# A two-layer diffusion trunk: layer 1's first modulation group is computed inside layer 0's MLP

## The chip, the cores and the metric

One core of one Trainium2 chip. The core has five engines that run at once, each through its own queue in order: TensorE (PE, matrix products into PSUM; its weight loads are shown as PEld), VectorE (DVE), ScalarE (ACT), GpSimd (POOL), and SyncE (SP), which here issues the DMAs. The metric is the device time of one execution in microseconds, median over runs.

## The reference, cut to what matters

Two layers. In each, six modulation vectors are computed from a small condition (one vector for the 1024 latent tokens, one for the 128 context tokens); they scale and shift two normalised inputs and gate two outputs. The mixer (four head groups: two kinds of attention, a gated delta net, a long convolution) comes first, then a squared-ReLU MLP.

```python
def trunk_layer(x, cond, P, mixer):
    mod = jnp.einsum('bd,de->be', jax.nn.silu(cond), P['w_ada']) + P['b_ada']
    sh1, sc1, gt1, sh2, sc2, gt2 = jnp.split(mod[:, None, :], 6, axis=-1)
    h = rms_norm(x, P['g_pre_mix']) * (1.0 + sc1) + sh1
    o, extra = mixer(h)
    x = x + gt1 * rms_norm(o, P['g_post_mix'])
    h = rms_norm(x, P['g_pre_mlp']) * (1.0 + sc2) + sh2
    m = jnp.einsum('blf,fd->bld', jnp.square(jax.nn.relu(jnp.einsum('bld,df->blf', h, P['mlp_w1']))), P['mlp_w2'])
    x = x + gt2 * rms_norm(m, P['g_post_mlp'])
    return x, extra
```

The model width is 1024, the MLP's 4096. `w_ada` is 1024 x 6144 for each layer. The modulation depends on the condition and the weights alone, so it can be computed at any time before it is used.

## The kernel before

**Modulation.** `ada(l, g)` computes a third of layer `l`'s modulation, group `g`: (sh1, sc1), (gt1, sh2) or (sc2, gt2). The 2048 columns of `w_ada` of a group are cut into four slices of 512. A group has eight steps, one for each 128 rows of `w_ada`. A step loads four tiles `wada` of 128 x 512 (256 KB each, line 392, on SP's queue) and makes four products with the condition `cst` (128 x 32) in float32. Product `h` writes partitions 32h to 32h+31 of one PSUM tile `ada`, and accumulates there over the eight steps. After the last step ScalarE copies the tile to `adarow` (L398), TensorE transposes it in four pieces to `adat` (L229), and VectorE adds the bias into `mod` (L406).

**Who runs the groups.** Layer 0's group 0 runs in the lead. The others run in the mixer: `adas()` inside `layer` waits until the input projections are done and then runs, step by step, the layer's groups 1 and 2, and in layer 0 also layer 1's group 0. `run_timed` weaves this with `rest()` (projections, hyena, attention) and `other()` (the gated delta net) by a virtual clock for each. In attention `S` is the first pass that finds each query's largest score (its maximum goes through DRAM, `mscr`, and back into `Q`), `ST` the scores for the weights, `den` the sums of the weights, `O` the weighted values. After attention comes the output projection, `op`.

**The MLP.** `mlp` works in blocks; a block has two slices of 128 of the 4096 hidden columns (`j`). It runs 15 blocks, and `mlp_last` does the sixteenth. A block loads `w1` and `w2` of its two slices (`load_cols` and `load_rows`, lines 251 and 241: each a stage tile of 256 KB in tag T, then a cast of its high part by ScalarE, L253 and L242, and of the rest by VectorE, L232). Its first half makes `hid` (24 products of 384 columns for each of six pieces), with ReLU and square by ScalarE and VectorE (L1821 to L1823); its second half makes `mo` (18 tiles of 512 columns, six products each), which VectorE adds to `acc` (L1839).

**Buffers.** SBUF tags used here: T, 4 buffers, the stage tiles of `w1` and `w2`, and the `wada` tiles; L, 8 buffers, which hold the `w1` of just one block; C, 5 buffers, where the `w2` of one block stand in layer 0. PSUM: P, 4 banks, for `mo`, `ada`, `adat` and most others; q and O, 2 each, for `hid`.

**What sets the order.** The program is traced as a list of instructions. A planner then orders each engine's instructions by that list's order and by a simulated timeline, takes a tile's buffer when an earlier tile of the tag is free, and adds the semaphores; each engine then runs its queue in that order. `with tc.issue_after(i)` makes what is traced in the block stand behind instruction `i` on the same engine; it adds no wait. `self.last` is the last product traced by `mm`.

Of the kernel before, what the change touches and what calls it, by code (L numbers as in the profile page):

```python
# [19 lines left out]
DEPTH = 2  # L20
# [138 lines left out]
def bc(ap, n):  # L159

    return ap.unsqueeze(len(ap.shape)).broadcast_to(list(ap.shape) + [n])


class Trunk:
# [220 lines left out]
    def ada(self, l, g, tag="T"):  # L385

        nc = self.nc
        ps = self.P(name="ada")
        for kt in range(8):
            for h in range(4):  # L390
                w = self.H(name="wada", tag=tag[h % len(tag)])
                i = nc.sync.dma_start(out=w, in_=self.I["w_ada"][l, kt, :, g * 2048 + h * 512:g * 2048 + (h + 1) * 512])
                self.mm(ps[32 * h:32 * h + 32, :], self.cst[:, kt], w, kt == 0, kt == 7)
            if l == g == 0:
                self.lead = i
            yield
        row = self.H(name="adarow")
        nc.scalar.copy(out=row, in_=ps)  # L398
        pt = self.P((4, 2, 2, 32), name="adat")
        for b in range(4):  # L400
            self.tr(pt[:, b], row[:, b * 128:(b + 1) * 128])

        for half in range(2):
            o = self.mod[l][:, g, half * 4:half * 4 + 4]
            b = self.bada[l].rearrange("p (g s h b) -> p g s h b", g=3, s=2, h=2)[:, g, :, half].rearrange("p s b -> p b s")
            nc.vector.tensor_tensor(out=o, in0=pt[:, :, :, half, 0:2], in1=bc(b, 2), op=ALU.add)  # L406
        yield
# [1397 lines left out]
    def mlp(self, l, hi, lo):  # L1805
        nc = self.nc
        acc = []
        for b in range(15):
            us, w1s, w2s = [], [], []
            for j in (2 * b, 2 * b + 1):  # L1810
                w1s.append(self.load_cols(self.I["w1"][l, j], "w1"))
                w2s.append(self.load_rows(self.I["w2"][l, j * 128:(j + 1) * 128], "w2", [self.small] * 2))
                us.append((self.W(dt=F32R, name="uh", tag=self.big), self.W(dt=F32R, name="ul", tag="C" if j % 2 else self.big)))
            for c0, n in NCH:
                s = slice(c0, c0 + n)
                for w1, (uh, ul) in zip(w1s, us):
                    ps = self.P(name="hid", tag="Q")
                    for k in range(8):
                        self.mm3(ps[:, :n], w1(k), [hi[k][:, s], lo[k][:, s]], k == 0, k == 7)
                    r = self.H(name="relu")  # L1820
                    nc.scalar.activation(out=r[:, :n], in_=ps[:, :n], func=AF.Relu)  # L1821
                    nc.vector.scalar_tensor_tensor(out=r[:, :n], in0=ps[:, :n], scalar=0.0, in1=r[:, :n], op0=ALU.max, op1=ALU.mult)  # L1822
                    nc.scalar.copy(out=uh[:, s], in_=r[:, :n])  # L1823
                    self.lo_of(ul[:, s], r[:, :n], uh[:, s])
                if b == 0 and c0 < 768:
                    yield
            if b == 0:
                acc = [self.W((1024,), name="acc", tag=self.big) for _ in range(9)]
            for t in range(9):
                ts = slice(t * 128, t * 128 + 128)  # L1830
                for n in range(2):
                    ns = slice(512 * n, 512 * n + 512)
                    ps = self.P(name="mo")
                    for j in range(2):
                        self.mm3(ps, [x[:, ts] for x in us[j]], [x[:, ns] for x in w2s[j]], j == 0, j == 1)
                    if b == 0:
                        nc.vector.tensor_copy(out=acc[t][:, ns], in_=ps)
                    else:
                        nc.vector.tensor_tensor(out=acc[t][:, ns], in0=acc[t][:, ns], in1=ps, op=ALU.add)  # L1839
            yield acc  # L1840
# [203 lines left out]
    def layer(self, l):  # L2044


        I, nc = self.I, self.nc
# [26 lines left out]
        w = self.first_weights(l)  # L2074
# [23 lines left out]
        g, be = self.gdn_shared(l, gab, self.gdn_tag)  # L2098
# [5 lines left out]
        def until(x):  # L2104
            while x not in self.done:
                yield 1

        def adas():
            yield from until("proj")
            for a in ((l, 1), (l, 2)) + (((l + 1, 0),) if l + 1 < DEPTH else ()):  # L2110
                for _ in self.ada(*a):
                    yield 5

# [21 lines left out]
        def ahead(g):  # L2135
            while True:
                with self.tc.high_priority(300):
                    t = next(g, "end")
                if t == "end":
                    return  # L2140
                yield t
        run_timed((rest(), 1.5), (ahead(other()), GD), (adas(), 1))
        self.small, self.other = R[0][-1], R[1][-1]
        op = self.out_proj(l, R[1])
# [19 lines left out]
        for ts in range(7):  # L2164
            g = op([ts])
            out = next(g)
# [3 lines left out]
        g = op([7, 8])  # L2170
        out = next(g)
        self.run((g, 1), (group(0, xs[0:3]), 1), (group(1, xs[3:6]), 1))
        g = self.mlp(l, hi, lo)
# [75 lines left out]
```

## Time and profile before

| | us |
|---|---|
| median of 3 runs | 3819.6 |
| lowest, highest | 3818.95, 3856.05 |
| the profiled execution | 3818.92 |
| its span, first to last instruction | 3817.1 |

Times in the rows are microseconds from the start of the span. Names such as `L213` are lines of the kernel before; L213 is the helper that makes all products, so products are told apart by their tiles. `x8` counts instructions; a float32 product counts as two matmul instructions, one of the fp32r kind (`hid`, `mo`, `pj`) as one. In brackets stands how long the engine had been idle, and for what. Layer 0's MLP runs about 1150 to 1850 us, layer 0's attention about 690 to 1005, layer 1's about 2600 to 2885.

### The profile page before, as it was taken

To read this page: it belongs to the slowest core of one execution; us is meant where nothing else is said; L and a number is where in the kernel's file an instruction comes from. 1 tells how busy PE (TensorE), PEld (TensorE's weight loads), DVE (VectorE), ACT (ScalarE), POOL (GpSimd) and SP (SyncE) were. 2 spreads that over 40 slices of the span, in tenths; PEclk is the share of its full clock that TensorE was granted. 3 is DMA by queue.
4 is the path that set the end of the run, shared out by engine and by line. 5 is a ranking of instruction groups with operands and counts; after the bars stand their busy time and mean duration, and the time that the engine had idled before them with its cause. 6 is when DMAs were issued, how large, how long until landed. Compare 5 with 4: busy or idle time off the path is not lost. (4 is left out here: it accounts for less than half of the span.)

```text
span 3817.1 us, 58820 instructions
## 1 busy us (share of the span) xinstructions
PE 3530.3 (92%) x22478; PEld 2940.8 (77%) x22478; DVE 2236.0 (59%) x4583; ACT 1367.0 (36%) x2972; POOL 710.1 (19%) x710
## 2 busy tenths in 40 slices
PE   7989888799899999999989798787989999999998
PEld 4879774366689999999968787545656899999997
DVE  5765567677645444444586674767774544444446
ACT  5434343265543122212364334323664422222112
POOL 1152531013420000000131633211143200000003
PEclk9998889799999999999999898897989999999999
DMA  5346476832421111111334465755414211111113
GB/s 203 115 115 158 137 266 201 240 84 60 141 86 48 42 45 44 35 44 45 100 104 129 112 151 151 262 185 167 101 40 138 72 45 45 45 45 45 39 39 122
DMA packets 364677, 405.40 MB, mean 106 GB/s; under 512 B 115816, under 2 KB 237158, under 8 KB 364395
## 3 DMA queue, kind: packets, MB, share of 16 engines
q1 hardware_dynamic: 364394, 401.63, 35.1%
q8 instruction: 177, 2.90, 0.3%
q14 instruction: 106, 0.86, 0.1%
HBM read 298.34 MB, written 103.19 MB: 105 GB/s over the span
## 5 line engine op out<-in xcount | busy, mean ns | idle before, releaser
L213 PE MATMUL hid<-hT,w1h 128*128 128x384 f32 x3072 | 786.6, 335 | 0.1
L213 PE MATMUL pj<-hT,wah 128*128 128x384 f32 x2112 | 575.8, 351 | 10.4 <-ACT wah L253 4.2
L1839 DVE TENSOR_TENSOR acc<-acc,mo 128x512 f32<-128x512 f32 x504 | 345.9, 686 | 391.9 <-PE mo L213 391.9
L213 PEld LDWEIGHTS hid<-hT,w1h 128*128 128x128 f32 x3072 | 557.6, 188 | 14.4 <-ACT h L481 1.1
L213 PE MATMUL hid<-hT,w1l 128*128 128x384 f32 x1536 | 514.1, 335 | 0.0
L213 PE MATMUL mo<-w2h,ul 128*128 128x512 f32 x1116 | 435.0, 392 | 0.0
L213 PE MATMUL mo<-w2h,uh 128*128 128x512 f32 x1080 | 422.7, 391 | 0.0
L213 PE MATMUL mo<-w2l,uh 128*128 128x512 f32 x1080 | 422.7, 391 | 0.0
L213 PEld LDWEIGHTS pj<-hT,wah 128*128 128x128 f32 x2112 | 396.3, 196 | 23.3 <-issue 7.5
L213 PE MATMUL pj<-hT,wal 128*128 128x384 f32 x1056 | 368.2, 349 | 0.7 <-DVE wal L232 0.7
L242 ACT CAST w2h<-w 128x512 fp32r<-128x512 f32 x128 | 70.3, 619 | 732.7 <-PE mo L213 728.5
L269 POOL TENSOR_TENSOR postr<-postr,mhalf 128x1 f32<-128x1 f32 x36 | 22.3, 622 | 1564.1 <-DVE postr L268 1563.7
L213 PEld LDWEIGHTS hid<-hT,w1l 128*128 128x128 f32 x1536 | 288.3, 188 | 2.5
L213 PEld LDWEIGHTS mo<-w2h,ul 128*128 128x128 f32 x1116 | 209.6, 188 | 46.1
L662 POOL TENSOR_TENSOR e<-e,e 128x512 f32<-128x512 f32 (+1 forms) x120 | 162.2, 1353 | 445.3 <-ACT e L651 267.4
L213 PEld LDWEIGHTS mo<-w2h,uh 128*128 128x128 f32 x1080 | 202.8, 188 | 37.5
L213 PEld LDWEIGHTS mo<-w2l,uh 128*128 128x128 f32 x1080 | 202.7, 188 | 36.5
L232 DVE TENSOR_TENSOR el<-e,eh 128x512 fp32r<-128x512 f32 (+1 forms) x252 | 202.3, 820 | 32.2 <-ACT eh L653 30.3
L213 PEld LDWEIGHTS pj<-hT,wal 128*128 128x128 f32 x1056 | 206.4, 195 | 4.6 <-issue 2.0
L1822 DVE SCALAR_TENSOR_TENSOR relu<-hid,relu 128x384 f32<-128x384 f32 x180 | 99.4, 553 | 167.2 <-ACT relu L1821 167.2
L213 PE MATMUL ada<-wada,cst 128*32 128x512 f32 x384 | 137.0, 688 | 46.9 <-DMA wada<-in_w_ada 46.7
L1821 ACT ACTIVATE relu<-hid 128x384 f32<-128x384 f32 x180 | 87.8, 488 | 184.8 <-PE hid L213 184.8
(502 smaller groups left out, 6318.1 us busy)
## 6 DMA issues: line engine op xcount, KB each, us to landing
w<-in_w SPq DMA_DIRECT2D x256, 256.0 KB
wada<-in_w_ada SPq DMA_DIRECT2D x192, 256.0 KB
wa<-in_wa SPq DMA_DIRECT2D x88, 256.0 KB
x<-xres SPq DMA_DIRECT2D x21, 512.0 KB
x<-in_x SPq DMA_DIRECT2D x18, 512.0 KB
Q<-rscr SPq DMA_DIRECT2D x32, 288.0 KB
o<-oscr SPq DMA_DIRECT2D x18, 512.0 KB
xres<-x SPq DMA_DIRECT2D x36, 256.0 KB
```

What stands on the lines that cost most here:

```text
L213: self.last = self.nc.tensor.matmul(out, l, r, start=start, stop=stop, skip_group_check=True)
L232: self.nc.vector.tensor_tensor(out=lo, in0=x, in1=hi.bitcast(F32), op=ALU.subtract)
L242: self.nc.scalar.copy(out=hi[:, q], in_=st)
L269: self.nc.gpsimd.tensor_tensor(out=out, in0=out, in1=self.bcs(self.mhalf[:out.shape[0]], out.shape), op=ALU.pow)
L662: self.nc.gpsimd.tensor_tensor(out=acc, in0=acc, in1=e, op=ALU.add)
L1821: nc.scalar.activation(out=r[:, :n], in_=ps[:, :n], func=AF.Relu)
L1822: nc.vector.scalar_tensor_tensor(out=r[:, :n], in0=ps[:, :n], scalar=0.0, in1=r[:, :n], op0=ALU.max, op1=ALU.mult)
L1839: nc.vector.tensor_tensor(out=acc[t][:, ns], in0=acc[t][:, ns], in1=ps, op=ALU.add)
```

## The change

Layer 1's group 0 leaves layer 0's mixer and goes into layer 0's MLP. There `beside` runs one step in each of the blocks 1 to 8: its four loads are traced at the opening of the block, behind the block's own loads; its four products in the middle, behind the block's last `hid`, the one of the fourth tile first and the other three behind it. At the opening of block 9 come the copy, the transposes and the adds. In layer 1 `beside` is empty. For all other groups `ada` now takes a step's four tiles and traces its four loads first and its four products after them, where before each load was followed by its product.

```diff
@@ ada(self, l, g, tag="T")
         for kt in range(8):
+            w = [self.H(name="wada", tag=tag[h % len(tag)]) for h in range(4)]
             for h in range(4):
-                w = self.H(name="wada", tag=tag[h % len(tag)])
-                i = nc.sync.dma_start(out=w, in_=self.I["w_ada"][l, kt, :, g * 2048 + h * 512:g * 2048 + (h + 1) * 512])
-                self.mm(ps[32 * h:32 * h + 32, :], self.cst[:, kt], w, kt == 0, kt == 7)
+                i = nc.sync.dma_start(out=w[h], in_=self.I["w_ada"][l, kt, :, g * 2048 + h * 512:g * 2048 + (h + 1) * 512])
+            if g == 0 and l:
+
+                yield
+                with self.tc.issue_after(self.last.ins):
+                    self.mm(ps[96:128, :], self.cst[:, kt], w[3], kt == 0, kt == 7)
+            with self.tc.issue_after(self.last.ins) if g == 0 and l else contextlib.nullcontext():
+                for h in range(3 if g == 0 and l else 4):
+                    self.mm(ps[32 * h:32 * h + 32, :], self.cst[:, kt], w[h], kt == 0, kt == 7)
             if l == g == 0:
                 self.lead = i
             yield
@@ mlp(self, l, hi, lo)
         acc = []
+        beside = self.ada(l + 1, 0) if l + 1 < DEPTH else iter(())
         for b in range(15):
...
+            if b:
+                next(beside, None)
             for c0, n in NCH:
...
+            if b:
+                next(beside, None)
             if b == 0:
                 acc = [self.W((1024,), name="acc", tag=self.big) for _ in range(9)]
@@ layer(self, l)
         def adas():
             yield from until("proj")
-            for a in ((l, 1), (l, 2)) + (((l + 1, 0),) if l + 1 < DEPTH else ()):
+            for a in ((l, 1), (l, 2)):
                 for _ in self.ada(*a):
                     yield 5
```

## Rows read from the trace of the kernel before

**Rows 1.** Page, busy time of each engine over the span.

```profile
PE 3530.3 (92%) x22478; PEld 2940.8 (77%) x22478; DVE 2236.0 (59%) x4583; ACT 1367.0 (36%) x2972; POOL 710.1 (19%) x710
```

**Rows 2.** Windows, layer 0's MLP: stretch, length, busy us, PEclk, DMA share, GB/s.

```profile
1300.00:1350.00 50.00, 50.00 (x254) 45.50 (x253) 23.82 (x38) 10.29 (x20) 0.00 (x0) 1.00 0.13 43
```

**Rows 3.** Waits, 1200 to 1300 us: total us, times, longest.

```profile
DVE acc L1839 <- PE mo L213: 28.7, 31, 1.8
```

**Rows 4.** Windows of `ada` alone: stretch, length, PE, PEld, ACT busy, PEclk, DMA, GB/s.

```profile
700.00:730.30 30.30, 9.34 (x25) 1.22 (x26) 0.00 (x0) 0.68 0.95 280
730.30:770.00 39.70, 18.58 (x40) 2.35 (x38) 0.58 (x1) 1.00 0.71 204
```

**Rows 5.** Waits of TensorE, 700 to 730.3 us.

```profile
PE ada L213 <- DMA wada<-in_w_ada: 6.1, 4, 4.2
```

**Rows 6.** Timeline of TensorE in layer 0's attention: start us, us, engine, line, operation.

```profile
756.40 1.05 PE L213 MATMUL ada<-wada,cst 128*32 128x512 f32 x2
757.38 0.62 PE L213 MATMUL S<-K,Q 96*128 96x384 f32 x2
```

**Rows 7.** Timeline of TensorE at the end of layer 1's projections.

```profile
2428.66 0.33 PE L213 MATMUL pj<-hT,wal 128*128 128x384 f32 x1
2428.83 0.51 PE L213 MATMUL pj<-hT,wah 128*128 128x384 f32 x2
2429.18 0.34 PE L213 MATMUL pj<-hT,wal 128*128 128x384 f32 x1
2429.44 1.06 PE L213 MATMUL ada<-wada,cst 128*32 128x512 f32 x8
```

**Rows 8.** Timeline of TensorE in layer 0's hyena.

```profile
650.22 1.06 PE L213 MATMUL ada<-wada,cst 128*32 128x512 f32 x8
651.21 1.13 PE L213 MATMUL iz<-Y,inv 128*128 128x256 f32 x4
```

**Rows 9.** Timeline of TensorE, the end of the group that moves.

```profile
767.98 0.66 PE L229 MATMUL adat<-ident,adarow 128*128 128x128 f32 x4 [0.31 <-ACT adarow L398]
```

**Rows 10.** By tile: ns min/median/max, first and last start us; each layer's attention.

```profile
L213 PE MATMUL S<-K,Q x100: 275/340/689, 687.0 to 851.0; 96*128 96x384 f32 x96, 96*128 96x128 f32 x4
...
L213 PE MATMUL den<-e,ones x528: 269/273/423, 730.3 to 1006.6; 128*32 128x128 f32 x176
...
L213 PE MATMUL op<-woh,oh x144: 387/389/473, 1005.1 to 1109.4; 128*128 128x512 f32 x144
...
L213 PE MATMUL S<-K,Q x100: 275/387/689, 2598.9 to 2732.4; 96*128 96x384 f32 x96, 96*128 96x128 f32 x4
...
L213 PE MATMUL den<-e,ones x528: 272/296/423, 2631.4 to 2886.2; 128*32 128x128 f32 x176
...
L213 PE MATMUL op<-woh,oh x144: 387/389/499, 2885.3 to 2994.5; 128*128 128x512 f32 x144
```

**Rows 11.** Timeline of ScalarE in one block of layer 0's MLP.

```profile
1320.94 2.19 ACT L242 CAST w2h<-w 128x512 fp32r<-128x512 f32 x4 [25.34 <-PE mo L213]
...
1341.13 0.62 ACT L253 CAST w1h<-w 128x512 fp32r<-128x512 f32 x1
```

**Rows 12.** Timeline of TensorE around the same block.

```profile
1305.24 0.51 PE L213 MATMUL hid<-hT,w1h 128*128 128x384 f32 x2
...
1321.65 0.51 PE L213 MATMUL hid<-hT,w1h 128*128 128x384 f32 x2
...
1343.00 0.39 PE L213 MATMUL mo<-w2h,uh 128*128 128x512 f32 x1
```

**Rows 13.** Timeline of SP's queue, the same block's issues.

```profile
1322.32 1.52 SPq L251 DMA_DIRECT2D w<-in_w  x2
...
1338.15 2.41 SPq L251 DMA_DIRECT2D w<-in_w  x2
```

**Rows 14.** Timeline of VectorE, adds of `acc` in the same block.

```profile
1345.96 0.69 DVE L1839 TENSOR_TENSOR acc<-acc,mo 128x512 f32<-128x512 f32 x1
1347.32 0.69 DVE L1839 TENSOR_TENSOR acc<-acc,mo 128x512 f32<-128x512 f32 x1 [0.67 <-PE mo L213]
```

## Prediction, made before the changed kernel was run

> **What bounds the kernel now.** I read the page first: TensorE is busy for 92% of the span [rows 1], so in most stages TensorE's own work is the time, and what is added there is paid. The question is where that holds, so I read the windows next. In the MLP of layer 0 a window of 50 us has TensorE busy for all 50 us, at the full clock (1.00 is 2.4 GHz), VectorE under half, ScalarE a fifth, DMA 0.13 [rows 2]. The list of waits of that stretch has no wait of TensorE at all; the others wait for it, VectorE's adds of `acc` for `mo` 31 times in 100 us, 1.8 us at most [rows 3]. One block is 144 products `hid` and 108 products `mo`, 252 together; at 254 in 50 us a block takes 49.6 us. So the MLP is a stream of TensorE work without a hole: any product that is put into it lengthens the kernel by its own length.
>
> The group that moves, layer 1's group 0, runs in layer 0's mixer between 700 and 770 us. The windows of its products alone give 9.34 + 18.58 = 27.9 us of TensorE [rows 4] for 32 products, 8 steps of 4 (a product here is two matmul instructions), and before 730 us TensorE stood 6.1 us waiting for their loads [rows 5]. Why 28 us for so little: the timeline shows products alone among attention's products, one (x2) taking from 756.40 to 757.38, 0.98 us [rows 6]. The four products of a step write four different quarters of the output's partitions, and where all four are queued together they share the array: x8 stands with 1.06 us, and the next product starts 0.99 us after the first [rows 7, 8]. So the same step costs about 1 us together and about 4 us one by one. That is the lever of this change.
>
> **What the change removes.** The 64 instructions, their 32 loads and the waits. Bounds: at most the whole of it, 27.9 + 6.1 + 0.66 for the four transposes [rows 4, 5, 9] = 34.7 us. To see how much of that sets the end, there is a twin: layer 1 runs the same attention with two groups only, both over before its first `S`. From the first `S` to the first `op` layer 0 takes 1005.1 - 687.0 = 318.1 us, layer 1 2885.3 - 2598.9 = 286.4 us [rows 10]: 31.7 us less. It splits at the first `den` and the last `S`. First `S` to first `den`: 43.3 against 32.5 us, 10.8 less. First `den` to last `S`: 120.7 against 101.0 us, 19.7 less. Last `S` to first `op`: 154.1 against 152.9. Of the group, 9.3 us of TensorE and 6.1 us of waiting lie in the first part, 18.6 us and the transposes in the second [rows 4, 5], so the twin's differences sit where the group sits. The second part is TensorE's own time and I count it as sure; in the first part TensorE also waits, DMA is at 0.95 [rows 4], and layer 1 may do it faster for another reason. So 19.7 us is the lower bound, 34.7 the upper, and I take 31, next to the twin. The diff also lets the remaining groups ask for four tiles at once before their four products; loads and products are on different queues and their order on each stays, so I put that at nothing; it is bounded by the 0.98 us of a lone product either way for each step, and nothing in the rows says which way.
>
> **What the change adds on TensorE.** Eight steps, one in each of blocks 1 to 8, behind the block's last `hid`. By then (below) all four tiles are there, so they go in one run. From a dense stream into it: the product before starts at 2429.18, the step at 2429.44; the same kind of product takes 0.17 us to the next (2428.66 to 2428.83), so 0.09 us is lost [rows 7]. Out of it 0.99 us [rows 8]. A step is 1.08 us, 8 steps 8.6 us. Block 9 adds four transposes of 0.66 us in all with a wait of about 0.3 us before them [rows 9]: 1 us. Together 9.6 us. The copy `adarow` and the two small adds `mod` lie on ScalarE and VectorE, which wait for TensorE in that stage (ScalarE once 25.3 us a block [rows 11]); without that cover they'd cost under 1 us. Lower bound of the cost 8 x 0.99 + 0.4 = 8.3 us; upper bound, products that don't share, 8 x (4 x 0.98 + 0.09) + 1 = 33 us. I take 9.6, since the rows with x8 are this very form.
>
> The row says that eight instructions take 1.06 us where two take 1.05 [rows 6 to 8], so four products cost no more than one. The Trainium skill ("TensorE: Matmul & The Clock Gate", Measured speedup vs the span model) gives less for four tiles, 3.07 times instead of 4. By that a step would be 4 x 0.98 / 3.07 = 1.28 us (my estimate from that page) and the sum 1.6 us more. The trace disagrees here and decides. The page "TensorEngine Tiling (Array Packing)" of the Trainium skill, Key Properties, says that a change of the tiling mode drains the engine, which speaks against 16 such changes inside a dense stream; this trace shows 0.09 us for the way in.
>
> **What the change adds on the queues.** A step takes all four buffers of tag T, which the MLP's own loads use. Before, in a block that begins with `hid` at 1321.65 [rows 12], ScalarE casts the last four `w2` tiles at 1320.94 [rows 11], the buffers come free, and SP loads the next block's `w1` at 1322.32 and a second pair of `w1` at 1338.15 [rows 13]. Now the step's four loads stand at 1322 instead. A pair of tiles issued at 1338.15 was there when its cast ran at 1341.13, 3.0 us later [rows 11, 13], so four are there by about 1330, 13 us ahead of the middle of the block at 1343.00 [rows 12]. The 32 loads move past nothing else on SP there; DMA is at 0.13 [rows 2], where around the group it is at 0.95 and 0.71 [rows 4]. What is late next: all eight loads for the next block wait for the products, so they start near 1344. The first pair of `w1` lands at about 1347, is cast, the second by about 1351, done near 1353. The next block's `hid` begins at 1321.65 + 49.6 = 1371, 18 us later. But before, a few `hid` of the next block stand already among `mo`: the first at 1305.24, that is 11.8 us after that block's middle (1343.00 - 49.6 = 1293.4) [rows 12]. For such early ones only 2 us are left. I count nothing, since the planner places them by when their weights come; the price if it errs is rival B. The step's output holds one of four PSUM buffers P over eight blocks. `mo` fills one in 1.36 us and VectorE empties it in 0.69 us [rows 14]; with three left VectorE may be 2 x 1.36 - 0.69 = 2.0 us late, before 3.4. Nothing of it shows while VectorE is on time.
>
> **Sum.** -31 + 9.6 = -21.4 us on the profiled run of 3818.9 us: 3797.5. That run is 0.7 us below the median of the runs shown, so about 3798.
>
> **Rivals.**
> A, the first part is not won: attention's own loads on SP and the round trip of its maxima through DRAM set its length, not the group. Then only 19.7 us go, and 19.7 - 9.6 leaves 10 us: 3809. For it: DMA at 0.95 there with the group's loads only a part of the traffic [rows 4]. Against it: the 6.1 us that TensorE waited for just those loads [rows 5].
> B, the other side, the weights come late in the MLP. The next block's `w1` is cast in the `mo` half now; VectorE's part of the cast waits in its queue for the landing, the adds of `acc` are queued behind it, and TensorE runs out of P buffers. Two landings of 3.0 us, less the 2.0 us that three buffers cover, are 4.0 us a block, 32 in eight: -21.4 + 32 = 10.6 slower, 3830. It decides from 21.4 / 8 = 2.7 us a block. For it: only 2 us for early `hid`, one buffer less. Against it: ScalarE, VectorE and DMA are more idle than busy there.
> C, the four products don't run together in the MLP: 33 - 31 = 2 us slower, 3821. Against it stand all the x8 rows.
> D, the planner orders the rest of the mixer otherwise once the group is gone, or puts the step elsewhere in a block: either sign, some 20 us about the forecast.
>
> **How the numbers follow.** Forecast 0.60 (its own range 3793 to 3805: a gain of 27 to 34.7 less a cost of 8.3 to 12), A 0.14, B 0.14, C 0.05, D 0.07. The range 3787 to 3828 holds the forecast, A, C and most of D, and leaves out B's upper half. A measurement of this kernel can tell about 1%, 38 us, from no change: faster by more would need more than the whole group for nothing, 0.03; slower by more needs B at twice its price or a bad D, 0.08; within 1% 0.89.
>
> **What would show it.** Right: no `wada` load between 700 and 770; first `S` to first `op` of layer 0 near 287 us; in blocks 1 to 8 one row of `ada` x8 with 1.06 us right behind the last `hid`, no wait for `wada`; these blocks 50.7 us, block 10 and after 49.6. Wrong: a wait of TensorE for a `w1` cast or for `acc` in the MLP (B), rows of x2 there (C), 43 us still from first `S` to first `den` (A).

## The result and the profile after

The changed kernel takes 3849.0 us (median of 20 executions, 3830.3 to 3867.1); the kernel before, on the same chip in turn with it, 3820.8 us (20 executions, 3805.6 to 3856.1). The ratio is 1.0059, with a 95% interval of 1.0036 to 1.0082: slower by 0.6%, where 0.6% faster was forecast. The means of the same executions are 3848.2 and 3826.3 us, 21.9 us apart. The profiled execution took 3865.5 us, its span is 3863.7 us: it is the second slowest of the 20, so the profiled pair, 46.6 us apart by span, shows more than the usual difference.

The first line of the page of the changed kernel, busy time of each engine, against [rows 1]:

```profile
PE 3571.5 (92%) x22478; PEld 2978.2 (77%) x22478; DVE 2230.5 (58%) x4583; ACT 1368.9 (35%) x2972; POOL 708.1 (18%) x710
```

TensorE has exactly as many instructions as before, 22478, and is 41 us longer busy. The same work takes longer: that is where to look.

First the MLP. Timeline of TensorE in the changed kernel: two steps of the group, the turn from `hid` to `mo` in two later blocks without a step, and SP's issues around the second step.

```profile
1210.63 0.34 PE L213 MATMUL hid<-hT,w1l 128*128 128x384 f32 x1
1210.90 1.06 PE L213 MATMUL ada<-wada,cst 128*32 128x512 f32 x8
1211.89 0.50 PE L213 MATMUL mo<-w2h,uh 128*128 128x512 f32 x1
1212.23 0.39 PE L213 MATMUL mo<-w2l,uh 128*128 128x512 f32 x1
...
1262.08 1.07 PE L213 MATMUL ada<-wada,cst 128*32 128x512 f32 x8
...
1720.08 0.39 PE L213 MATMUL mo<-w2h,uh 128*128 128x512 f32 x1
...
1769.86 0.39 PE L213 MATMUL mo<-w2h,uh 128*128 128x512 f32 x1
...
1248.24 3.76 SPq L392 DMA_DIRECT2D wada<-in_w_ada  x4
1263.16 0.80 SPq L251 DMA_DIRECT2D w<-in_w  x2
```

All eight steps stand as x8 with 1.06 or 1.07 us. A block with a step takes 51.18 us (1210.90 to 1262.08), one without 49.78 us (1720.08 to 1769.86). The loads stand 13.8 us ahead of the products, and the next block's `w1` is issued right behind the products, as forecast. In this MLP TensorE waits for nothing. From the first to the last `hid` it takes 802.7 us instead of 791.2.

Now attention. By tile, layer 0, then layer 1, against [rows 10]:

```profile
L213 PE MATMUL S<-K,Q x100: 275/388/689, 685.1 to 842.2; 96*128 96x384 f32 x96, 96*128 96x128 f32 x4
L213 PE MATMUL den<-e,ones x528: 269/296/423, 723.2 to 1022.4; 128*32 128x128 f32 x176
L213 PE MATMUL op<-woh,oh x144: 387/389/632, 1021.2 to 1126.5; 128*128 128x512 f32 x144
...
L213 PE MATMUL S<-K,Q x100: 224/344/689, 2602.7 to 2759.1; 96*128 96x384 f32 x96, 96*128 96x128 f32 x4
L213 PE MATMUL den<-e,ones x528: 272/296/423, 2638.2 to 2932.5; 128*32 128x128 f32 x176
L213 PE MATMUL op<-woh,oh x144: 389/389/632, 2931.1 to 3041.1; 128*128 128x512 f32 x144
```

First `S` to first `op`: layer 0 takes 336.1 us (before 318.1, forecast 287), layer 1, which the prediction did not touch, 328.4 (before 286.4). The windows of the three parts (first `S`, first `den`, last `S`, first `op`), layer 0 and then layer 1, say why. Columns: stretch, length, busy us of PE, PEld, DVE, ACT, POOL, then PEclk, DMA share, GB/s. Before:

```profile
687.00:730.30 43.30, 30.53 (x105) 16.55 (x103) 28.80 (x75) 6.54 (x13) 5.24 (x2) 0.68 0.94 269
730.30:851.20 120.90, 120.05 (x735) 74.71 (x733) 82.17 (x139) 64.85 (x119) 20.49 (x15) 1.00 0.47 123
851.20:1005.10 153.90, 139.46 (x804) 89.78 (x803) 115.27 (x212) 96.08 (x198) 58.85 (x46) 0.93 0.25 63
2598.90:2631.40 32.50, 25.79 (x96) 17.99 (x97) 27.97 (x59) 3.62 (x9) 0.00 (x0) 0.73 0.84 242
2631.40:2732.60 101.20, 100.83 (x670) 70.27 (x670) 73.93 (x120) 64.74 (x118) 20.58 (x15) 0.97 0.29 68
2732.60:2885.30 152.70, 136.74 (x802) 89.02 (x801) 113.88 (x211) 95.19 (x197) 60.73 (x46) 0.93 0.25 64
```

After:

```profile
685.10:723.20 38.10, 22.99 (x77) 16.86 (x75) 27.67 (x73) 6.45 (x13) 5.25 (x2) 0.55 0.85 248
723.20:842.40 119.20, 117.52 (x752) 81.70 (x751) 87.79 (x145) 71.56 (x130) 22.28 (x15) 0.94 0.29 72
842.40:1021.20 178.80, 163.47 (x748) 106.08 (x747) 109.70 (x205) 91.18 (x188) 56.56 (x45) 0.73 0.21 55
2602.70:2638.20 35.50, 20.58 (x66) 14.32 (x64) 28.10 (x73) 6.25 (x13) 5.26 (x2) 0.56 0.93 266
2638.20:2759.30 121.10, 119.47 (x759) 83.11 (x760) 91.20 (x147) 70.45 (x128) 22.09 (x15) 0.93 0.30 78
2759.30:2931.10 171.80, 154.72 (x748) 101.34 (x748) 109.83 (x204) 90.68 (x188) 58.08 (x45) 0.77 0.22 57
```

Look at layer 0's last part: 748 instructions after, 804 before, and yet 25 us longer, with a granted clock of 0.73 instead of 0.93. It stands idle for as long as before (178.80 - 163.47 = 15.3, before 14.4 us). In all these traces the granted clock stands at one of two levels, 1.00 (2.4 GHz) or 0.50 (1.2 GHz), so the time at half clock in a stretch is 2 x (1 - PEclk) x length. For layer 0's attention it comes to 145 us after and 48 before, for layer 1's to 126 and 44 (from the unrounded clock; the two digits of PEclk give 1 us more here and there). And the instruction counts of the parts differ in both layers (layer 1: 96, 670, 802 before, 66, 759, 748 after): the planner has laid out attention anew in both.

By stage the span's 46.6 us are: layer 0's attention +18.0, the MLP +11.5, from its last `hid` to layer 1's first `S` -24.8 (691.8 before, 667.0 after), layer 1's attention +42.0, the rest together -0.1.

### The profile page after: what moved, and what is told of

The parts are those of the page before. It is cut to its first block, busy times and chain, and to the rows that moved or that the text cites. A ratio compares the mean times of both kernels' runs of the same rounds, so it can differ in the third digit from the quotient of the medians.

```text
span 3863.7 us, 58828 instructions
## 1 busy us (share of the span) xinstructions
PE 3571.5 (92%) x22478; PEld 2978.2 (77%) x22478; DVE 2230.5 (58%) x4583; ACT 1368.9 (35%) x2972; POOL 708.1 (18%) x710
## 5 line engine op out<-in xcount | busy, mean ns | idle before, releaser
L213 PEld LDWEIGHTS pj<-hT,wah 128*128 128x128 f32 x2112 | 393.4, 195 | 39.1 <-ACT hc L526 24.8
L232 DVE TENSOR_TENSOR wal<-wa,wah 128x512 fp32r<-128x512 f32 x88 | 63.8, 729 | 170.6 <-ACT wah L253 139.7
```

What stands on the lines that cost most here:

```text
L213: self.last = self.nc.tensor.matmul(out, l, r, start=start, stop=stop, skip_group_check=True)
L232: self.nc.vector.tensor_tensor(out=lo, in0=x, in1=hi.bitcast(F32), op=ALU.subtract)
```

## The experiments

Theory 1: the change makes the planner order attention anew, and in the new order the granted clock stands at half for longer. Theory 2: the clock falls by chance, in any order. Theory 3: the loop that loads four tiles first costs. A table of all of them first. Each execution comes with its mean granted clock, so the time at half clock is known for each; it and the time are means over all executions of a kernel (medians and ratios stand with the experiments). The kernel before, 73 executions run beside the experiments in four series (their means are 3827.5 to 3831.8 us): 3829.3 us, 400 us at half clock (for the 20 run beside the change, against which it is 21.9 us slower, the clocks are not at hand). "Work" is what remains of the difference if each us at half clock is taken as 0.5 us lost, and in brackets at 0.4.

| kernel | executions | us against before | us at half clock against before | work |
|---|---|---|---|---|
| the change | 20 | +18.9 | +82 | -22 (-14) |
| e4, the change, old loop | 10 | +20.5 | +87 | -23 (-14) |
| e1, new loop alone | 10 | -2.5 | -9 | +2 (+1) |
| e2, group left out | 6 | -21.3 | +20 | -31 (-29) |
| e3, group in both places | 5 | +22.1 | +28 | +8 (+11) |
| e5, products at the block's end | 4 | +58.4 | +109 | +4 (+15) |
| e6, late w_out casts | 10 | +30.0 | +94 | -17 (-8) |
| e7, both | 4 | +47.4 | +100 | -3 (+8) |
| e8, before with late w_out casts | 10 | +23.0 | +28 | +9 (+12) |
| e9, maxima spread | 10 | +10.1 | +60 | -20 (-14) |
| e10, spread, late w_out casts | 10 | +9.5 | +40 | -10 (-7) |
| e11, maxima bunched | 10 | +14.0 | +40 | -6 (-2) |

The factor is measured, and lies nearer to the one of the brackets: within a kernel, execution against execution (194 of them, all kernels), a us at half clock goes with 0.41 us of time, correlation 0.95. And across the 23 attentions without the group, of both layers, in all the traces with the maxima (below), length = 269 us + 0.464 x us at half clock, none off by more than 7.0 us; the five with the group lie 25 to 29 us above that line. The Trainium skill ("TensorE: Matmul & The Clock Gate", HAM oscillation) prices such time at half its length; by that the 82 us would be 41 (an estimate from that page). By the 0.41 of these executions, which decides, they are 34.

**Parts of the change.**

e1, the kernel before with the loop alone:

```diff
+            w = [self.H(name="wada", tag=tag[h % len(tag)]) for h in range(4)]
             for h in range(4):
-                w = self.H(name="wada", tag=tag[h % len(tag)])
-                i = nc.sync.dma_start(out=w, ...)
-                self.mm(ps[32 * h:32 * h + 32, :], self.cst[:, kt], w, kt == 0, kt == 7)
+                i = nc.sync.dma_start(out=w[h], ...)
+            for h in range(4):
+                self.mm(ps[32 * h:32 * h + 32, :], self.cst[:, kt], w[h], kt == 0, kt == 7)
```

> The kernel before with one part of the change alone: a step's four tiles and four loads first, its four products after them, all groups still in the mixers. The planned order of all TensorE products other than ada is that of the kernel before. Theory 1 (the change makes the planner order attention anew in both layers, and in the new order the granted clock falls to half): no new order here, so the time of the kernel before, within 10 us, and attention of layer 0 (first S to first op) within 10 us of 318. Theory 2 (the clock falls by chance in any order of this stage): attention differs from the profiled run of before by up to 25 us, at a clock that differs as much. Theory 3 (the loads-first loop itself costs): 15 us slower or more.

Measured: 3830.9 us, ratio 0.9997 (0.9968 to 1.0026). TensorE's order is that of the kernel before in every stage. Theory 3 falls.

e2, the kernel before with the group left out:

```diff
-            for a in ((l, 1), (l, 2)) + (((l + 1, 0),) if l + 1 < DEPTH else ()):
+            if l + 1 < DEPTH:
+                nc.vector.memset(self.mod[l + 1][:, 0], 0.0)
+            for a in ((l, 1), (l, 2)):
```

> The kernel before with layer 1's group 0 left out of the mixer altogether (its modulation is set to zero), so only the removal. The order of layer 0's mixer is then that of the changed kernel, layer 0's MLP and almost all of layer 1 keep the order of before. Theory 1: layer 0's attention goes the way it went in the changed kernel, first S to first op near 336 us at a clock of 0.66 in part of it, and the whole is 5 to 20 us slower than before although work was taken out. Theory 2: anything from 31 us faster to 15 slower, with other places of half clock than in the changed kernel. The prediction's own step: 31 us faster.

Measured: 3805.8 us, ratio 0.9958 (0.9929 to 0.9988). TensorE's order in layer 0's attention is now that of the changed kernel (layer 1's nearly that of the kernel before). Layer 0's attention takes 319.8 us, not less than with the group, with 102 us at half clock. Its last part:

```profile
843.10:1005.70 162.60, 147.18 (x749) 95.25 (x748) 109.56 (x205) 89.12 (x186) 56.88 (x44) 0.82 0.24 60
```

So taking the group away is enough to lay out layer 0 anew, and there the clock takes back what the work gives. Theory 1 missed the sum: it expected 336 us there and the whole slower. What the profiled execution of e2 gains on the kernel before, 20.5 us, lies between layer 0's MLP and layer 1's first `S` (671.3 us, before 691.8), where the edit takes no work out. Why is not shown; 20 us less at half clock in that stretch are a part of it.

e3, the group computed in both places:

```diff
+    def ada(self, l, g, tag="T", queued=False):
+        beside = self.ada(l + 1, 0, queued=True) if l + 1 < DEPTH else iter(())
```

> Layer 1's group 0 is computed twice, in the mixer as before and in the MLP as in the changed kernel, so only the addition. Layer 0's mixer has the order of before, layer 0's MLP that of the changed kernel, and layer 1's projections and mixer come out in nearly the changed kernel's new order. Theory 1: layer 0's MLP 11 to 12 us longer, layer 1 about 18 us longer (1928 against 1910 us after layer 0's last hid), in sum 25 to 35 us slower than before. Theory 2: the MLP 11 to 12 us longer, layer 1 by chance. The prediction's own step: 10 us slower, layer 1 unchanged.

Measured: 3848.5 us, ratio 1.0064 (1.0037 to 1.0092). Layer 0's attention keeps its old order and takes 318.7 us with 48 us at half clock. The MLP is again 802.7 us. Layer 1's projections and attention, which the edit does not touch, stand nearly in the order of the changed kernel; attention there takes 334.7 us with 150 us at half clock, and its first `S` comes 669.7 us after the MLP's last `hid` (before 691.8). The last part of attention, layer 0 and layer 1:

```profile
851.40:1005.00 153.60, 139.28 (x805) 89.43 (x805) 115.23 (x212) 95.79 (x198) 58.66 (x45) 0.93 0.25 64
2744.60:2922.70 178.10, 164.38 (x749) 107.83 (x748) 108.85 (x204) 89.71 (x186) 57.87 (x45) 0.71 0.22 55
```

So it is the step in the MLP that lays out layer 1 anew.

e4, the change with the old loop for all other groups:

```diff
-            w = [self.H(name="wada", tag=tag[h % len(tag)]) for h in range(4)]
+            else:
+                for h in range(4):
+                    w = self.H(name="wada", tag=tag[h % len(tag)])
```

> The changed kernel with the old loop (a load, its product, four times) for all groups but the moved one. The order of TensorE's products other than ada is that of the changed kernel everywhere. Theory 1: as the changed kernel, 25 to 35 us slower than before, with half clock in the same places of attention as there. Theory 2: places of half clock other than in the changed kernel. Theory 3 (the loop costs): back to before or faster.

Measured: 3845.8 us, ratio 1.0061 (1.0028 to 1.0093): the changed kernel again, with its order throughout. It is also a second trace of that order: attention 313.5 us with 97 us at half clock in layer 0 (336.1 with 145 in the first trace), 322.6 with 121 in layer 1 (328.4 with 126). Chance has its share, as Theory 2 says.

**Where the clock falls.** In the changed kernel TensorE stops 10 us after layer 0's last `S`. Rows of VectorE and TensorE there, and windows around it:

```profile
850.39 2.38 DVE L232 TENSOR_TENSOR wol<-wo,woh 128x512 fp32r<-128x512 f32 x2
852.70 0.68 DVE L934 TENSOR_REDUCE smx<-sC 128x2 f32<-128x512 f32 x1
...
853.43 0.43 PE L213 MATMUL sS<-sK,sQ 64*128 64x384 f32 x1 [0.92 <-DVE smx L934]
...
850.00:855.00 5.00, 3.99 (x19) 2.42 (x17) 5.00 (x11) 4.19 (x9) 3.52 (x3) 1.00 0.71 190
855.00:860.00 5.00, 5.00 (x28) 2.86 (x26) 4.26 (x11) 2.25 (x5) 0.00 (x0) 0.61 1.05 214
860.00:885.00 25.00, 25.00 (x101) 14.90 (x101) 9.14 (x18) 9.52 (x17) 2.54 (x2) 0.50 0.42 102
885.00:890.00 5.00, 5.00 (x13) 3.94 (x12) 1.84 (x5) 2.22 (x4) 1.28 (x1) 0.50 0.00 0
```

VectorE casts `w_out` (2.38 us), the maximum `smx` of attention's fifth or sixth group of queries waits behind that, and TensorE's next small product `sS` waits 0.92 us for `smx` to free its PSUM buffer. Then the clock is at 0.50 for 34 us, though TensorE is busy without a hole. The kernel before has the casts 8 us later behind its last `S`, and no wait at this place. e5 to e11 vary what leads there.

e5, the step's products behind the block's `mo`, to give layer 1 its old order back; e6, the `w_out` casts held back behind the last `smx`; e7, both; e8, the late casts in the kernel before:

```diff
@@ mlp, e5 and e7: the second next() of a block
-            if b:
-                next(beside, None)
             if b == 0:
...
+            if b:
+                next(beside, None)
@@ out_proj, e6 to e8 (self.smx is the last reduction in swa_prep)
+        with self.tc.issue_after(self.smx.ins):
-        Wo = [self.load_rows(...) for k in range(8)]
+            Wo = [self.load_rows(...) for k in range(8)]
```

> The change with one line moved: the step's four products are queued behind the block's mo instead of in front of them. The work is the same, but layer 1's projections and attention now stand nearly in the order of the kernel before, while layer 0's mixer stands in the changed kernel's order. Theory 1 (the change costs through the orders that it brings about, most of it in layer 1, where the clock falls to half): layer 1's attention (first S to first op) back from 328 to about 286 us with about 46 us at half the clock, layer 0's still 314 to 336, the MLP 11 to 13 us longer than before; layer 1's way to its first S is again some 18 us longer, so the whole is 10 to 20 us under the changed kernel, about 3825 to 3840. Theory 2 (the clock falls by chance in any order): layer 1's attention stays at 320 to 335 us and the time is that of the changed kernel, 3849.

> The change, with the casts of the w_out tiles on VectorE held back until the last maximum of attention's second group of queries is taken, so that they no longer stand in front of the maxima for which TensorE waits 0.9 us. Theory 1 with this trigger (TensorE stops for those maxima, then the clock goes to half): the third part of attention, last S to first op, has a clock of 0.9 or more in both layers and takes about 153 us instead of 179 and 172, the whole is 25 to 45 us under the changed kernel, 3805 to 3825. Rival (the fall has another trigger than these waits): the third part stays at 165 to 180 us with a clock under 0.8, the time within 10 us of the changed kernel.

> Both edits: products behind the block's mo, and the w_out casts held back. Layer 1's attention stands nearly as in the kernel before, layer 0's in the order without the group and without the casts in front of the maxima. Theory 1: layer 0's attention 286 to 300 us, layer 1's 286 to 295, the MLP 11 to 13 us longer, the whole 3795 to 3810, which is under both kernels. Rival (another trigger): layer 0's attention 314 to 336 us as in the changed kernel, 3825 to 3840.

> The kernel before, with only the w_out casts held back. It is the control for the edit by itself: in layer 0 it leaves the order nearly as it is, in layer 1 the projections and the attention are ordered anew. Theory 1 (what matters is the order in which TensorE meets the waits): layer 0's attention 312 to 320 us as before; layer 1's goes by its new order, and if the casts are the trigger it takes 285 to 295 us, so 3815 to 3825 in all. Rival (any new order of layer 1 has the clock at half): layer 1's attention 320 to 335 us, 3845 or more.

Measured: e5 3887.0 us, ratio 1.0160 (1.0116 to 1.0204); e6 3860.4, 1.0076 (1.0035 to 1.0117); e7 3877.2, 1.0132 (1.0087 to 1.0177); e8 3850.5, 1.0079 (1.0044 to 1.0114). All four missed Theory 1's times. For e8 the rival came: its layer 1, laid out anew, takes 320.4 us with 106 us at half clock.

e5 and e7 showed the cause of rival B, weights that come late, at another place. Waits of TensorE in layer 0's MLP of e5:

```profile
PE hid L213 <- ACT w1h L253: 26.4, 8, 3.6
```

With the products at the end, the next block's `w1` comes late by 3.3 us in each of eight blocks, and the MLP takes 839.3 us, 36.6 more than in the changed kernel: the waits are 26.4 of it, and the MLP now has 31 us at half clock, where both kernels have none. The middle of the block is what keeps the change's MLP free of waits. Layer 1's attention in e5 and e7, in nearly the old order, still takes 304.0 and 299.6 us, with 90 and 66 us at half clock; for e5 about 286 with 46 was expected.

e6 took away the stop that it aimed at. Windows from the same place on in e6, and then in the kernel before (there the first line holds the part's only wait for `smx`, 0.61 us):

```profile
850.00:855.00 5.00, 4.25 (x26) 2.79 (x26) 4.63 (x9) 2.95 (x6) 2.52 (x2) 1.00 0.94 220
860.00:885.00 25.00, 25.00 (x155) 15.26 (x154) 17.37 (x33) 15.84 (x29) 3.92 (x3) 1.00 0.27 55
895.00:935.00 40.00, 40.00 (x119) 25.61 (x117) 18.64 (x42) 16.15 (x34) 12.17 (x10) 0.50 0.10 26
```

```profile
910.00:915.00 5.00, 4.39 (x19) 2.74 (x18) 3.38 (x9) 3.24 (x8) 2.23 (x2) 1.00 0.06 16
915.00:940.00 25.00, 24.60 (x128) 16.43 (x128) 22.54 (x50) 16.02 (x36) 12.35 (x11) 1.00 0.15 38
```

No fall at 855 now (TensorE waits there 0.74 us for another cast, `el`); it comes 40 us later, behind waits of 0.18 and 0.26 us for `smx`. Over the traces of the changed kernel and of e1 to e12: where TensorE waits 0.65 to 0.94 us for `smx` at 10 to 12 us after the last `S`, the clock falls in 9 of 11 attentions; with the late casts in 0 of 6, though TensorE waits there 0.51 to 0.75 us for `el`; but a later fall takes its place, and the sum is not better. The kernel before has its 0.61 us wait 60 us after the last `S`, without a fall in the first trace.

e9, the maxima of the last two groups spread (1.4 steps for each step of the attention beside); e10, that with late `w_out` casts; e11, bunched (2 steps); e12, the kernel before again:

```diff
-            for _ in weave([(main, 1), (preps[i + 1], PR)] + ...
+            for _ in weave([(main, 1), (preps[i + 1], PR if i < 3 else 1.4)] + ...
```

> The change, with the maxima of attention's last two groups of queries spread over the products: 1.4 steps of them to each step of the attention that runs beside them instead of 1.6. The work is the same, layer 1's projections stand as in the changed kernel, both mixers nearly so. Theory 1 with the waits of TensorE for these maxima as the trigger: fewer and shorter waits in the third part of attention (last S to first op), so fewer falls of the granted clock: half-clock time of each attention from 125 to 148 us down to 60 to 100, each us of it worth about 0.5 us, in all 25 to 45 us under the changed kernel, 3805 to 3825. Rival (the maxima are not the trigger): half-clock time as in the changed kernel, 3840 to 3860.

> The changed kernel with both edits: the maxima spread (1.4 steps), and the w_out casts on VectorE held back behind the last of them. Theory 1 with VectorE's delay as the trigger: the fall of the clock 10 us after the last S is gone in both layers and the one 55 us after it too, half-clock time 50 to 80 us for each attention, 3795 to 3815. Rival: as for the spread alone, with the time of the changed kernel or the 3860 that the late casts alone gave.

> The opposite of the spread: the changed kernel with 2 steps of the maxima of the last two groups to each step of attention instead of 1.6. Theory 1 with the waits as the trigger: more waits for the maxima in the third part, half-clock time of each attention 140 to 180 us, 3855 to 3885. Rival (the order of these steps does not matter): 3840 to 3860.

> The kernel before once more, for a second trace of the same order. Theory 1 (the order decides where the clock falls): third part of attention 153 to 154 us in both layers, half-clock time 45 to 55 us in layer 0 and 40 to 50 us in layer 1, span 3812 to 3820. Theory 2 (it falls by chance in any order): third part over 160 us in one of the layers, and the time then above 3830.

Measured: e9 3840.7 us, ratio 1.0020 (0.9986 to 1.0054); e10 3838.0, 1.0021 (0.9999 to 1.0042); e11 3842.6, 1.0021 (1.0004 to 1.0038). Theory 1's times were missed in all three. Spread and bunched came out alike, so how densely these steps stand does not decide; and all three lie nearer to the kernel before than the change does (1.0059), though their work is the change's. e12 took 3833.3 us, with layer 1 as before (286.1 us, 39 at half clock). Its layer 0, last part and the place of the 0.61 us wait:

```profile
846.90:1023.70 176.80, 163.58 (x804) 106.11 (x804) 114.84 (x212) 97.57 (x200) 57.88 (x46) 0.78 0.22 55
...
905.00:910.00 5.00, 4.39 (x15) 2.93 (x16) 1.89 (x9) 1.62 (x5) 0.89 (x1) 0.66 0.01 2
910.00:960.00 50.00, 50.00 (x150) 32.91 (x149) 24.39 (x56) 20.33 (x43) 12.72 (x12) 0.50 0.08 21
```

The same 804 instructions in the same order, the same busy 4.39 us of 5 around the same wait as before at 910: there the clock held, here it is at half for the next 50 us and more. So Theory 2 is half right: the order does not settle whether the clock falls in one execution. Theory 1 is right on the odds: of the eight attentions whose last part stands in exactly the old order, this one alone fell there, and the other seven have 15 to 20 us at half clock in that part; the seven in exactly the changed kernel's orders (its own two, e4's two, e3's layer 1, layer 0 of e2 and of e5) all have 49 to 102. Of three that stand nearly in the old order, e8's layer 0 held (14 us), and layer 1 of e5 and of e7 fell (63 and 42), so a small difference of order can be enough.

**Without the maxima.** Last, the waits for `smx` were taken away by leaving their work out: the maxima of the last two groups of queries, with zero as the shift of these softmaxes. (The ratio of weights doesn't depend on the shift, but nothing guards against overflow then. They are 48 products for each group, 96 in a layer; the expectation counts them twice.)

```diff
@@ swa_prep
-        for t in range(8):
...
-            V.tensor_reduce(out=mx[:, 1, :, t], in_=pc.rearrange("p i k c -> p i (k c)"), axis=AX.X, op=ALU.max)
-            yield
+        V.memset(mx, 0.0)
+        for _ in range(24):
+            yield
```

> The kernel before with the maxima of attention's last two groups of queries left out (96 small products for each of the two, their reductions and the waits for them; the shift is zero instead). It is one half of a pair with the next run. Theory A (the falls of the granted clock in the third part of attention come behind TensorE's waits for these maxima): no wait and no fall until late in that part, half-clock time 15 to 30 us under that of the kernel before in each layer, the time 30 to 50 us under it. Theory B (the clock falls in this part whatever is waited for): half-clock time as before, 10 to 30 us less time, which is the products' own.

> The changed kernel with the same maxima left out. Theory A: without these waits the changed kernel's orders cost no more clock than those of the kernel before, so both have half-clock times within 20 us of each other and what is left is the work: 15 to 25 us faster than the run above (31 for the group less 11 for the MLP). Theory B (the orders cost clock for another reason): half-clock time again 60 to 100 us above the run above, and the changed kernel is 10 to 30 us slower than it, as in the pair with the maxima.

> The kernel before with both left out, the maxima as above and layer 1's modulation group 0 (its modulation set to zero). Theory A: the group costs its work, about 31 us, so 26 to 36 us under the first of these three runs. Theory B: half-clock time 20 us and more above it, 10 to 20 us under it.

| | median | ratio to before | mean us | us at half clock |
|---|---|---|---|---|
| e13, before | 3778.7 | 0.9860 (0.9805 to 0.9916) | 3777.7 | 383 |
| e14, the change | 3772.4 | 0.9846 (0.9790 to 0.9903) | 3772.5 | 398 |
| e15, group left out | 3759.0 | 0.9812 (0.9747 to 0.9878) | 3757.8 | 391 |

Layer 0's attention, three parts, e13 and then e14:

```profile
687.80:731.50 43.70, 30.13 (x105) 16.58 (x103) 28.83 (x75) 6.56 (x14) 5.26 (x2) 0.69 0.92 265
731.50:852.10 120.60, 119.85 (x734) 74.66 (x733) 82.11 (x139) 64.80 (x119) 20.47 (x15) 1.00 0.48 123
852.10:985.80 133.70, 115.73 (x708) 76.59 (x708) 97.08 (x132) 93.78 (x197) 60.52 (x45) 0.92 0.29 73
```

```profile
684.30:723.90 39.60, 22.95 (x77) 16.88 (x74) 27.71 (x73) 6.45 (x14) 5.26 (x2) 0.53 0.87 246
723.90:846.70 122.80, 121.05 (x751) 83.27 (x751) 87.63 (x145) 71.60 (x130) 22.29 (x15) 0.91 0.29 70
846.70:978.30 131.60, 113.75 (x651) 76.37 (x649) 88.65 (x124) 87.75 (x185) 59.02 (x44) 0.86 0.30 74
```

The last part no longer collapses: 131.6 against 133.7 us, where it was 178.8 against 153.9. The two kernels differ by 15 us at half clock instead of 82, and the mean of the changed one is 5.2 us lower (95% interval of the difference from the spread of four and four: -13.1 to +2.7) instead of 18.9 higher: no longer slower, but not clearly faster either. Theory A had the difference in half-clock time right (within 20 us), but not the gain (15 to 25). It also expected less half clock in both attentions of e13 than before: layer 0's has the same 48 us, layer 1's 67 instead of 44. Layer 1 of e13 was itself laid out anew by leaving the maxima out, and the changed order still has more half clock in the first two parts of layer 0 (0.53 and 0.91 against 0.69 and 1.00). e15 against e13, the whole price of the group: 19.9 us (14.3 to 25.5), where 26 to 36 was expected. e14 beats both kernels, by its missing maxima far more than by the change.

## Why the prediction was wrong

**The MLP was right.** Forecast 9.6 us, measured 11.5 (802.7 - 791.2). x8 at 1.06 us, no wait for `wada`, no wait for `w1`: as written. The block grew by 51.18 - 49.78 = 1.40 us, not 1.08, and the four transposes in block 9 cost 0.1 us, not 1, so two sizes were off against each other. The way in costs 0.27 - 0.17 = 0.10 us (1210.63 to 1210.90), close to the 0.09; the first `mo` behind the step takes 0.34 us to the next instead of 0.23. The last 0.2 us are probably the early `hid` among `mo`, which stand in shorter and more pieces; that is not shown. The Trainium skill ("TensorEngine Tiling (Array Packing)", Key Properties) says that a change of the tiling mode drains the engine; both of these 0.1 us agree with it, as small prices. Rivals B and C did not come. B's cause is real where the products stand half a block later: in e5 TensorE waits 3.3 us a block, near the 4.0 written down, but on another way, `hid` for ScalarE's cast of `w1` and not `mo` for a P buffer. So the nearness of the two sizes is luck.

**The work removed was near.** -31 was taken, with 19.7 to 34.7 as bounds. At equal half-clock time the attentions with the group lie 27 us above those without. e2's work, -31 (-29), is the forecast's number in part by luck: some of it lies behind layer 0's MLP, where nothing was taken out. The whole change's work is -22 at 0.5, but -15 at the 0.41 that was measured; forecast was -21.4. The other term that the prediction put at nothing, the loop that loads four tiles first, was nothing (e1). No `wada` load is left between 700 and 770. The first part did not keep its 43 us either (38.1), so A did not come as written.

**What failed is the step from work to time, the twin.** Layer 1's 286.4 us was taken as what layer 0 would take without the group, as if nothing but the group would change. The twin is 286.4 us long with its own order and its 44 us at half clock. In the prediction's three parts layer 0 should have taken 32.5, 101.0 and 152.9 us; it took 38.1, 119.0 and 179.0 (before 43.3, 120.7 and 154.1). The 19.7 us of the second part, which were counted as sure, came to 1.7, and the third, which was to stay, grew by 25. Layer 0 did not get the twin's order: its second part has 752 instructions, the twin's 670. It got one with 97 to 145 us at half clock in the two traces, and 269 + 0.464 x 145 = 336 us is what was measured, 336.1. The prediction used PEclk to tell that the MLP runs at the full clock; the same column in the twin's windows (0.73, 0.97, 0.93) said that 44 of its 286 us ran at half. The prediction had no term for it. Over all executions, 82 us more at half clock are +34 us at 0.41, and with the -15 of work they make the +19 of the means.

**The second half of it was not in the prediction at all.** It followed the step into layer 0's MLP and no further. Eight steps there laid out layer 1's projections and attention anew (e3): in the profiled pair its first `S` came 24.8 us sooner after the MLP and its attention took 42.0 us longer, 17.2 in all. The longer attention goes with its 82 us more at half clock. The sooner start cannot be put down to the new order alone: e2, nearly in the old one there, has most of it.

Rival D named the mechanism, for layer 0's mixer alone, at 0.07 and "some 20 us"; by the means the miss is 43 us (+21.9 against -21.4). It deserved more: every edit in this study that took something out of layer 0's mixer or put something into its MLP changed an order that it did not mean to change.

**What is open.** Why one order has better odds than another. It isn't only how long TensorE waits for `smx` (0.61 us held eight times and fell once in the old order; 0.17 and 0.26 us fell in e4), nor how densely the steps stand (e9, e11). What TensorE runs around these waits, many small products, was not varied by itself. Leaving the maxima out brought most of the difference down, but laid out both layers anew as well, so it does not separate the waits from the rest of the order. No run has an attention without the group in layer 0's old order, so order and group were not separated there; in layer 1, where no work is added or taken, they are (e3).

## What to carry to other kernels

Where a planner orders the queues, taking work out or putting it in is also a new order for everything behind it, two stages away too: compare the order of the stages that the edit does not mean, before counting on a twin. Count a stage's time at half clock as a term of its own, 2 x (1 - granted clock) x length; a us of it went with 0.41 to 0.46 us of time here. Removed work may come with more time at half clock, as here: compare kernels at equal half-clock time to see what an edit did, and their means to see what it brought.

## What was not expected of the hardware

- Behind a wait of 0.92 us the granted clock stood at 0.50 for 34 us, and in e12 behind one of 0.61 us for more than 50 us, while TensorE shows as busy without a hole.
- The same order, the same wait and the same busy share came with the full clock in one execution (before, 910 to 940) and with half in another (e12, 910 to 960). The 73 executions of the kernel before lie between 350 and 479 us at half clock, and within a kernel that time and the length of an execution go together with a correlation of 0.95.
- Four products into four quarters take 1.06 us between dense streams, in all eight steps, where they had taken TensorE some 3.5 us a step one by one [rows 4].
